# A hybrid decoder layer on one core: the first head's two weight tiles are multiplied chunk of tokens by chunk of tokens instead of tile by tile

## The chip, the core and the metric

The kernel runs on one core of a Trainium2 chip. The metric is the device time of one execution in microseconds (us). A core has five engines, each with its own in-order instruction queue: TensorE (PE in the profile, with its weight loads shown apart as PEld), VectorE (DVE), ScalarE (ACT), GpSimd (POOL) and SyncE (SP, which here only issues DMAs). They wait for one another by semaphores.

## What is computed

One layer of a hybrid decoder over a prompt of 1024 tokens and 32 sample tokens (8 sequences of 4), 1056 tokens in all, width 1024. The part around the change:

```python
h = _rmsnorm(x, norm1)                       # 1056 x 1024
z = h @ w_in                                 # columns: hq, hf, hi, hog, aq, ak, av, iq, ik, iw, ga, gb
# HGRN2 branch, 4 heads of 128
logf = jnp.logaddexp(jnp.log(lb), jnp.log1p(-lb) + jax.nn.log_sigmoid(hf))
o, s_new = _hgrn2(hq, -jnp.expm1(logf), hi, logf, s0)
o = _rmsnorm(o, hg_norm) * jax.nn.silu(hog)
# then sparse attention with an indexer, two gates, w_o, a squared-ReLU MLP, a last norm
```

For each head the HGRN2 branch takes four products of `h` with 128 columns of `w_in`: `hi` (the input, called `whi` in the trace), `hog` (the output gate, `whog`), `hq` and `hf`.

## The kernel before

**Stages.** The tokens are normed in nine blocks of 128 (the ninth has 32). For each block ACT squares and sums (L205), DVE scales (`ht`, L214), PE transposes the block in eight 128x128 pieces (`hTp`, L218), ACT casts the result into the high part `hh` (L219) and DVE subtracts to get the low part `hl` (L220). `hh` and `hl` hold `h` transposed: 8 slices of the width by 1056 tokens. Then come the four HGRN2 heads, the indexer's scores and the search for the top 256 keys, four heads of sparse attention with the sample tokens' attention beside them, the two branch projections, `w_o`, and the MLP.

**A product.** `proj` (L150) loads a weight tile of 1024 x 128 (`wload`, L132; ACT casts its high part and DVE subtracts the low part), and walks over three chunks of 352 tokens (`CUTS`). For each chunk `gemm3` (L142) issues 24 matmuls, three for each of the 8 slices of the width (high by high, L147; high by low, L148; low by high, L149), into one PSUM bank of the tag `g`, which has two banks. `evac` then empties the bank. Chunk 0 needs the token blocks 0 to 2, chunk 1 blocks 2 to 5, chunk 2 blocks 5 to 8.

**The first head.** The weights of `whi` and `whog` are loaded and split while the blocks are normed (L207, `first_w`). In the loop over heads `proj` is called for `whi` (evacuated by an ACT copy to `vT`, L375), the result is transposed back (`tokp`, L385), and then `proj` is called for `whog` (ACT takes the sigmoid `sgo`, L400, and DVE multiplies it into `sil`, L401). The transposes of the raw input (`xTp`, L233, into a PSUM tag `t` of two banks, copied by ACT at L235) are written between. The PSUM tag `s` (two buffers) serves `hTp`, `tokp` and others.

**What sets the order.** Instructions are not executed in the order of the text. A list scheduler places them on each engine's queue by readiness in its own estimate and by priority (the `tc.high_priority()` blocks go ahead), and each queue then runs strictly in that order. So an instruction that waits holds all those behind it on its engine, and a change in one place can change the order that the scheduler finds much later.

Of the kernel before, what the change touches and what calls it, by code (L numbers as in the profile page):

```python
# [10 lines left out]
F32 = mybir.dt.float32  # L11
# [3 lines left out]
AF = mybir.ActivationFunctionType  # L15
ALU = mybir.AluOpType
# [6 lines left out]
T = NP + NS  # L23
CH = 352
# [13 lines left out]
CUTS = (0, 352, 704, 1056)  # L38
# [14 lines left out]
C_HQ, C_HF, C_HI, C_HOG, C_AQ, C_AK, C_AV, C_IQ, C_IK, C_GA, C_GB = (  # L53
    0, 512, 1024, 1536, 2048, 2560, 3072, 3584, 4096, 4168, 5192)
# [37 lines left out]
def hybrid_step(ctx: ExitStack, tc, x_prompt, x_sample, cache_k, cache_v, cache_idx_k, state_hgrn,  # L92
# [3 lines left out]
    nc = tc.nc  # L96
# [5 lines left out]
    sm = ctx.enter_context(tc.tile_pool(name="sm", bufs=1))  # L102
    up = ctx.enter_context(tc.tile_pool(name="up", bufs=1))
    psum = ctx.enter_context(tc.tile_pool(name="psum", bufs=2, space=PSUM))
    U = Units(up, N_UNITS)

    def ps_g(name):
        return psum.tile([128, 512], F32, name=name, tag="g", bufs=2)

    def ps_t(name):  # L110
        return psum.tile([128, 512], F32, name=name, tag="t", bufs=2)
# [17 lines left out]
    hh = big.tile([128, 8, T], F32R, name="hh", tag="hh")  # L129
    hl = big.tile([128, 8, T], F32R, name="hl", tag="hl")  # L130


    def wload(rows, c0, nk, m, name):
        raw = wp.tile([128, nk, m], F32, name=name + "r", tag="wr", bufs=1)
        nc.sync.dma_start(raw, rows[:, c0:c0 + m].rearrange("(k p) m -> p k m", p=128))
        wh = wp.tile([128, nk, m], F32R, name=name + "h", tag="wh", bufs=2)
        wl = wp.tile([128, nk, m], F32R, name=name + "l", tag="wl", bufs=2)
        with tc.high_priority():
            nc.scalar.copy(wh, raw)  # L139
            nc.vector.tensor_tensor(wl, raw, wh.bitcast(F32), op=ALU.subtract)  # L140
        return wh, wl

    def gemm3(ps, ws, xs):
        n = len(ws)
        for k in range(n):
            (wh, wl), (xh, xl) = ws[k], xs[k]
            nc.tensor.matmul(ps, wh, xh, start=(k == 0), stop=False)  # L147
            nc.tensor.matmul(ps, wh, xl, start=False, stop=False)  # L148
            nc.tensor.matmul(ps, wl, xh, start=False, stop=(k == n - 1))  # L149

    def proj(c0, m, name, evac, after=None, w=None):
        wh, wl = w or wload(w_in[0], c0, 8, m, name)
        for c, (a, b) in enumerate(zip(CUTS, CUTS[1:])):
            sl = slice(a, b)
            ps = ps_g(name)[:m, :b - a]
            gemm3(ps, [(wh[:, k, :], wl[:, k, :]) for k in range(8)],
                  [(hh[:, k, sl], hl[:, k, sl]) for k in range(8)])
            with tc.high_priority():
                evac(ps, sl, c)
            if after:  # L160
                after()

    def rstd_of(ss, n, scale, name):
        rt = sm.tile([128, 3, 9], F32, name=name, tag="rs", bufs=2)
        v, r, t = (rt[:ss.shape[0], a, :n] for a in range(3))
        nc.vector.tensor_scalar(v, ss, scale, EPS, op0=ALU.mult, op1=ALU.add)
        nc.scalar.activation(r, v, AF.Sqrt)
        nc.vector.reciprocal(r, r)

        nc.vector.scalar_tensor_tensor(t, r, -0.5, r, op0=ALU.mult, op1=ALU.mult)  # L170
        nc.vector.tensor_tensor(t, t, v, op=ALU.mult)
        nc.vector.scalar_tensor_tensor(r, t, 1.5, r, op0=ALU.add, op1=ALU.mult)
        return r
# [19 lines left out]
    first_w = None  # L193
    for grp in GROUPS:
# [13 lines left out]
        if not first_w and grp[-1] >= FIRST_W:  # L208
            first_w = [wload(w_in[0], C_HI, 8, 128, "whi"), wload(w_in[0], C_HOG, 8, 128, "whog")]
# [122 lines left out]
    def gate_tile(after=None):  # L332
        w, j = gates.pop(0)

        def ev(ps, sl, c):
            gst = sm.tile([128, CH], F32, name="gst", tag="c352", bufs=2)
            nc.scalar.copy(gst, ps)
            nc.scalar.dma_start(sg_d[w, j][:, sl], gst)
        proj((C_GA, C_GB)[w] + j * 128, 128, "wgt", ev, after)
# [32 lines left out]
    tails = []  # L372
    for h in range(4):
        vT = U.get([128, T], F32, "vT")
        proj(C_HI + h * 128, 128, "whi", lambda ps, sl, c: nc.scalar.copy(vT[:, sl], ps),  # L375
             w=first_w[0] if h == 0 else None)

        vk = U.get([128, 8, 128], F32, "vk")
        vks = sm.tile([32, 128], F32, name="vks", tag="s128", bufs=2)
# [12 lines left out]
        if tails:  # L392
            tail(*tails.pop())

        sil = U.get([128, T], F32, "sil")

        def ev_og(ps, sl, c):
            sg_ = sm.tile([128, CH], F32, name="sgo", tag="c352", bufs=2)
            sg_ = sg_[:, :sl.stop - sl.start]
            nc.scalar.activation(sg_, ps, AF.Sigmoid)  # L400
            nc.vector.tensor_tensor(sil[:, sl], ps, sg_, op=ALU.mult)  # L401
        proj(C_HOG + h * 128, 128, "whog", ev_og, w=first_w[1] if h == 0 else None)
        q = U.get([128, T], F32, "q")
        proj(C_HQ + h * 128, 128, "whq", lambda ps, sl, c: nc.scalar.copy(q[:, sl], ps))
        b = U.get([128, T], F32, "b")
# [68 lines left out]
        for li, B in enumerate(LEVELS):  # L474
# [23 lines left out]
            ps = ps_t("lev")  # L498
# [56 lines left out]
    for t0, t1_ in ((0, 5), (5, 9)):  # L555
        ps = ps_t("tkp")
# [47 lines left out]
    for i in range(2, 8):  # L604
# [3 lines left out]
        w = L if small else L // 2  # L608
# [3 lines left out]
        for kind in (DOTS_S if small else DOTS_L):  # L612
# [8 lines left out]
            for ps in bk:  # L621
                h, o = todo.popleft()
# [410 lines left out]
    for step in SEQ.split():  # L1033
        op, n = step[0], int(step[1:] or 0)
# [139 lines left out]
    for j in (0, 4, 1, 5, 2, 6, 3, 7):  # L1174
        x1 = X1[j] = U.get([128, T], F32, f"x1_{j}")
        nc.gpsimd.dma_start(x1, xT_d[j])
        wh, wl = wload(w_o[0], j * 128, 8, 128, "wo")
# [3 lines left out]
        for c in range(NCH):  # L1181
            sl = slice(c * CH, (c + 1) * CH)
            ps = ps_g("po")[:, :CH]
# [11 lines left out]
        if j == 7:  # L1195
# [3 lines left out]
            for c in range(4):  # L1199
                sl = slice((c % 2) * TH + (c // 2) * TC, (c % 2) * TH + (c // 2 + 1) * TC)  # L1200
# [5 lines left out]
        if j >= 4:  # L1206
            kp = j - 4
            dst = {}
            for n_, q in enumerate(ORDER):
                w = kp * 7 + n_  # L1210
# [67 lines left out]
    def bank(i, q, c):  # L1278

        if q in ("P1", "P6", "P7", "P4"):  # L1280
            if (i, 0) not in BANK:
                t = ps_s("pua")
                BANK[i, 0] = [t[:, e, :TC] for e in range(2)]
            return BANK[i, 0][c]
        k = 1 if q == "P2" else 2
        if (i, k) not in BANK:
            BANK[i, k] = [(ps_g("pub") if k == 1 else ps_t("puc"))[:, :TC] for _ in range(2)]
        return BANK[i, k][c]
# [24 lines left out]
    for g, (i, q) in enumerate(SEVEN):  # L1313
        if q == "P2":
            hd[i] = [U.get([128, T], F32, f"hd{e}") for e in range(2)]
        for c in range(2):
            sl = slice(c * TC, (c + 1) * TC)
            s2 = slice(TH + c * TC, TH + (c + 1) * TC)
            product(g, c, (3,) if g in (0, 1, 3) else range(4))
            ps, u1 = bank(i, q, c), 3 * (i % 2)  # L1320
# [24 lines left out]
        if q in ("P2", "P7", "P4", "P3"):  # L1345
            e, sl = {"P2": (0, LO), "P7": (1, HI), "P4": (1, LO), "P3": (0, HI)}[q]
# [61 lines left out]
    for fb in range(8):  # L1408
        rows = w_down[0, fb * 512:(fb + 1) * 512, :]
        if fb < 7:  # L1410
            nxt = []
            for m2 in range(4):
                wh, wl = wd0 if fb == m2 == 0 else wload(rows, m2 * 256, 4, 256, "wd")
# [15 lines left out]
        else:  # L1429

            ws = []
            for m2 in range(4):
                raw = wp.tile([128, 4, 256], F32, name="wdr", tag="wr", bufs=1)
                nc.sync.dma_start(raw, rows[:, m2 * 256:(m2 + 1) * 256].rearrange("(k p) m -> p k m", p=128))
                wh = U.get([128, 4, 256], F32R, "wdh")
                wl = U.get([128, 4, 256], F32R, "wdl")
# [40 lines left out]
```

## Time and profile before

| | before |
|---|---|
| median of 3 runs (lowest to highest) | 1827.23 us (1824.29 to 1831.37) |
| the profiled execution's own time | 1815.77 us |
| its span, first to last instruction | 1814.1 us |
| mean granted TensorE clock | 0.987 of full speed |
| busy: PE, DVE, ACT, POOL | 96%, 63%, 43%, 10% of the span |

The profile is of one execution. Its rows give the start of an instruction or a group in us from the span's start, its length, the engine, the line, and the operands by the program's names. An engine's idle time before a group, and the instruction that ended it, stand in square brackets. The granted clock is 1 at 2.4 GHz and 0.5 at 1.2 GHz; values between are means over a stretch that has both.

### The profile page before, as it was taken

The numbers are of one execution on the slowest core, as the hardware profiler recorded it, in microseconds if no ns is written. First come the engines' busy times: TensorE is split into PE (matmuls) and PEld (weight loads), VectorE is DVE, ScalarE is ACT, GpSimd is POOL, SyncE is SP. The second block draws the span as 40 slices with busy tenths as digits, with TensorE's granted clock in tenths as the row PEclk, the third lists the DMA queues.
The fourth block names the chain that finished last, engine by engine and source line by source line (L and its number), as shares of the span: only waits on it lengthen the run. The fifth ranks groups of instructions, "written<-read, shape, count | busy, mean of one in ns | idle before, by whom it ended". The sixth has DMA issues, their size and how long they took to land.

```text
span 1814.1 us, 29069 instructions
## 1 busy us (share of the span) xinstructions
PE 1745.5 (96%) x11644; PEld 1689.5 (93%) x11644; DVE 1143.2 (63%) x2550; ACT 772.0 (43%) x1362; POOL 186.3 (10%) x212
## 2 busy tenths in 40 slices
PE   5999999999999999989999999999999999999997
PEld 5999999999999988877899999999999899999997
DVE  7185584746899897956647569655565634444435
ACT  5456475245577823244523455444444401111112
POOL 1100000023000014641100230000000000000000
PEclk9999999899999999989999999999999999999999
DMA  4421111231233224551553232233223712222212
GB/s 151 134 60 48 49 55 48 61 93 47 72 85 95 70 83 129 172 180 43 162 161 108 95 121 92 95 129 120 95 95 132 264 55 86 94 95 95 95 47 96
DMA packets 135847, 181.78 MB, mean 100 GB/s; under 512 B 9056, under 2 KB 111232, under 8 KB 135712
## 3 DMA queue, kind: packets, MB, share of 16 engines
q1 hardware_dynamic: 115232, 125.88, 21.6%
q0 software_dynamic: 13424, 44.87, 8.2%
q10 hardware_dynamic: 7056, 9.18, 1.4%
q8 instruction: 91, 1.49, 0.3%
q14 instruction: 44, 0.36, 0.1%
HBM read 128.96 MB, written 48.11 MB: 98 GB/s over the span
## 4 chain that ended last, share of the span: by engine, by line
PE 82%; DMA 6%; DVE 5%; issue 3%; POOL 2%; ACT 2%; SPq 0%; DVEq 0%; ACTq 0%; POOLq 0%
PE pua L1297 10%; PE pd L147 6%; PE pd L149 6%; PE pd L148 6%; PE puc L1297 5%; PE pub L1297 2%; PE lev L506 2%; PE wgt L147 2%; PE wgt L149 2%; PE wgt L148 2%; DMA qb<-q_d 2%; PE po L149 2%; DMA hdn<-hid_d 2%; PE po L148 2%; PE po L147 2%
## 5 line engine op out<-in xcount | busy, mean ns | idle before, releaser
L147 PE MATMUL pd<-hdn,wdh 128*128 128x352 f32 (+3 forms) x672 | 219.5, 327 | 3.2 <-DVE x L1405 3.1
L148 PE MATMUL pd<-hdn,wdh 128*128 128x352 f32 (+3 forms) x672 | 216.4, 322 | 0.0
L149 PE MATMUL pd<-hdn,wdl 128*128 128x352 f32 (+3 forms) x672 | 216.3, 322 | 0.0
L1405 DVE TENSOR_TENSOR x<-x,pd 128x352 f32<-128x352 f32 (+3 forms) x192 | 99.5, 519 | 177.7 <-PE pd L149 177.6
L147 PEld LDWEIGHTS pd<-hdn,wdh 128*128 128x128 f32 x672 | 126.7, 189 | 5.8 <-DVE x L1405 4.5
L148 PEld LDWEIGHTS pd<-hdn,wdh 128*128 128x128 f32 x672 | 126.9, 189 | 1.2
L149 PEld LDWEIGHTS pd<-hdn,wdl 128*128 128x128 f32 x672 | 126.6, 188 | 1.3
L147 PE MATMUL wgt<-hh,wgth 128*128 128x352 f32 x384 | 127.3, 331 | 0.0
L149 PE MATMUL wgt<-hh,wgtl 128*128 128x352 f32 x384 | 125.3, 326 | 0.0
L148 PE MATMUL wgt<-hl,wgth 128*128 128x352 f32 x384 | 125.1, 326 | 0.0
L139 ACT CAST wdh<-wdr 128x1024 fp32r<-128x1024 f32 x28 | 29.4, 1049 | 222.3 <-PE pd L148 210.9
L1297 PE MATMUL pua<-h2P,wuP 128*128 128x264 f32 x672 | 102.7, 284 | 0.0
L750 ACT ACTIVATE jkA<-sc,bstg 128x1024 bf16<-128x1024 bf16 (+5 forms) x93 | 87.1, 937 | 19.6 <-DVE bstg L769 6.8
L1297 PEld LDWEIGHTS pua<-h2P,wuP 128*128 128x128 f32 x672 | 90.4, 188 | 0.0
L745 DVE TENSOR_SCALAR_CACHE_REDUCE jkD<-sc,bstg 128x768 bf16<-128x768 f32 (+3 forms) x96 | 84.4, 879 | 1.1
L1297 PE MATMUL pua<-h2a,wuP 128*128 128x264 f32 x480 | 79.1, 286 | 1.7 <-ACT uu L1323 1.7
L147 PEld LDWEIGHTS wgt<-hh,wgth 128*128 128x128 f32 x384 | 72.6, 189 | 2.5 <-issue 1.7
L148 PEld LDWEIGHTS wgt<-hl,wgth 128*128 128x128 f32 x384 | 72.7, 189 | 1.4 <-issue 0.5
L149 PEld LDWEIGHTS wgt<-hh,wgtl 128*128 128x128 f32 x384 | 72.6, 189 | 1.4 <-issue 0.8
L1323 ACT COPY uu<-pua 128x264 f32<-128x264 f32 x96 | 36.3, 378 | 80.7 <-PE pua L1297 80.7
L1297 PEld LDWEIGHTS pua<-h2a,wuP 128*128 128x128 f32 x480 | 66.7, 188 | 3.0 <-ACT uu L1323 2.8
L1248 DVE TENSOR_TENSOR wuP<-ws,wuP 128x512 fp32r<-128x512 f32 x64 | 43.8, 687 | 39.8 <-ACT wuP L1247 39.4
(782 smaller groups left out, 4969.6 us busy)
## 6 DMA issues: line engine op xcount, KB each, us to landing
hid_d<-hd SPq DMA_DIRECT2D x32, 528.0 KB, 3.0
wu<-in_w_up_dram SPq DMA_DIRECT2D x32, 512.0 KB, 4.5
wdr<-in_w_down_dram SPq DMA_DIRECT2D x32, 512.0 KB, 3.4
hdn<-hid_d SPq DMA_DIRECT2D x28, 528.0 KB, 6.2
sg_d<-gst ACTq DMA_DIRECT2D x48, 176.0 KB, 2.0
wgtr<-in_w_in_dram SPq DMA_DIRECT2D x16, 512.0 KB, 4.2
qb<-q_d POOLq DMA_DIRECT2D x16, 512.0 KB, 4.6
wasg<-sg_d SPq DMA_DIRECT2D x8, 528.0 KB, 4.2
```

The costliest lines, as they stand in the source:

```text
L139: nc.scalar.copy(wh, raw)
L147: nc.tensor.matmul(ps, wh, xh, start=(k == 0), stop=False)
L148: nc.tensor.matmul(ps, wh, xl, start=False, stop=False)
L149: nc.tensor.matmul(ps, wl, xh, start=False, stop=(k == n - 1))
L506: nc.tensor.matmul(ps[:, c * 64:(c + 1) * 64], E[:, c * 128:(c + 1) * 128], mov(c * 128, (c + 1) * 128), start=True, stop=True)
L745: nc.vector.tensor_scalar(jkD[:, 0, :L], SC[i], s if isinstance(s, float) else s[:, a:a + 1], 0.0, op0=op, op1=ALU.add, accum_out=out[:, a ...
L750: nc.scalar.activation(jkA[:, 0, :(i + 1) * 128], src(i), AF.Sign, bias=thr[:, a:a + 1], accum_out=cnt[:, a:a + 1])
L1248: nc.vector.tensor_tensor(w[:, 1], src, w[:, 0].bitcast(F32), op=ALU.subtract)
L1297: nc.tensor.matmul(ps, w[:, a, k], x[:, b, sl], start=(q in "P1P2P5" and k == n_ == 0), stop=(k == 3 and n_ == 2), skip_group_check=True)
L1323: nc.scalar.copy(uu[c][:, {"P1": u1, "P6": 1, "P7": 2}[q]], ps)
L1405: nc.vector.tensor_tensor(x1[:, sl], x1[:, sl], ps, op=ALU.add)
```

## The change

A new function `proj_two` takes a list of products and walks over the three chunks in the outer loop and over the products in the inner one. For head 0 it is called with `whi` and `whog`, so the text has `whi` chunk 0, `whog` chunk 0, `whi` chunk 1, `whog` chunk 1, `whi` chunk 2, `whog` chunk 2. The other three heads keep the order they had. The same matmuls, evacuations and transposes are issued, and `sil` is allocated earlier for head 0.

```diff
+    def proj_two(ms):
+
+        for c, (a, b) in enumerate(zip(CUTS, CUTS[1:])):
+            sl = slice(a, b)
+            for name, evac, (wh, wl) in ms:
+                ps = ps_g(name)[:, :b - a]
+                gemm3(ps, [(wh[:, k, :], wl[:, k, :]) for k in range(8)],
+                      [(hh[:, k, sl], hl[:, k, sl]) for k in range(8)])
+                with tc.high_priority():
+                    evac(ps, sl, c)
...
         vT = U.get([128, T], F32, "vT")
-        proj(C_HI + h * 128, 128, "whi", lambda ps, sl, c: nc.scalar.copy(vT[:, sl], ps),
-             w=first_w[0] if h == 0 else None)
+
+        def ev_og(ps, sl, c):
+            sg_ = sm.tile([128, CH], F32, name="sgo", tag="c352", bufs=2)
...
+            nc.scalar.activation(sg_, ps, AF.Sigmoid)
+            nc.vector.tensor_tensor(sil[:, sl], ps, sg_, op=ALU.mult)
+
+        def ev_i(ps, sl, c):
+            nc.scalar.copy(vT[:, sl], ps)
+        if h == 0:
+            sil = U.get([128, T], F32, "sil")
+            proj_two([("whi", ev_i, first_w[0]), ("whog", ev_og, first_w[1])])
+        else:
+            proj(C_HI + h * 128, 128, "whi", ev_i)
...
-        proj(C_HOG + h * 128, 128, "whog", ev_og, w=first_w[1] if h == 0 else None)
+        if h:
+            sil = U.get([128, T], F32, "sil")
+            proj(C_HOG + h * 128, 128, "whog", ev_og)
```

The order that the scheduler finds is another on three engines. PE's queue before, where the first chunk of `whi` ends: the transposes of blocks 5 and 6 (`hTp` x16), one matmul of chunk 1, then the transposes of block 7.

```order
L148 MATMUL whi<-hl,whih 128x352
L149 MATMUL whi<-hh,whil 128x352
L218 MATMUL hTp<-ident,ht 128x128 x16
L147 MATMUL whi<-hh,whih 128x352
L218 MATMUL hTp<-ident,ht 128x128 x8
L148 MATMUL whi<-hl,whih 128x352
```

PE's queue now, from the end of the first chunk of `whog`. Ahead of these rows stand the 23 remaining matmuls of `whi` chunk 0, nine of `whog` chunk 0, the transposes of blocks 5 and 6, and eleven more of `whog`.

```order
L147 MATMUL whog<-hh,whogh 128x352
L148 MATMUL whog<-hl,whogh 128x352
L149 MATMUL whog<-hh,whogl 128x352
L244 MATMUL xTp<-idr,xt 128x128 x8
L229 MATMUL hTp<-ident,ht 128x128 x8
L244 MATMUL xTp<-idr,xt 128x128 x4
L147 MATMUL whi<-hh,whih 128x352
L148 MATMUL whi<-hl,whih 128x352
```

Fourteen matmuls of `whog` and eight transposes of the raw input now stand between the transposes of block 6 and those of block 7; before, one matmul stood there.

ACT's queue before, from the casts of blocks 4 to 7 on (`lbt` is the exponential for the forget gate's lower bound, `xT` the copies of the raw input's transposes):

```order
L219 CAST hh<-hTp 128x8x128 x4
L253 ACT_TABLE_LOAD
L253 ACTIVATE lbt<-lbt 128x8
L219 CAST hh<-hTp 128x8x32
L235 COPY xT<-xTp 128x512
L375 COPY vT<-whi 128x352
```

ACT's queue now, at the same place:

```order
L230 CAST hh<-hTp 128x8x128 x3
L390 ACT_TABLE_LOAD
L390 ACTIVATE sgo<-whog 128x352
L246 COPY xT<-xTp 128x512
L394 COPY vT<-whi 128x352
L246 COPY xT<-xTp 128x512
L264 ACT_TABLE_LOAD
L264 ACTIVATE lbt<-lbt 128x8
L230 CAST hh<-hTp 128x8x128
L246 COPY xT<-xTp 128x512
L230 CAST hh<-hTp 128x8x32
```

The sigmoid of `whog` chunk 0 with a table load, two copies of `xT`, the copy that frees `whi`'s bank and a second table load now stand ahead of block 7's cast. A third load stands further back, ahead of the second sigmoid; before, the two loads at this place and at the first sigmoid were all.

Between PE's 2754th and 4522nd instruction of 11047, which takes in the attention stage, the order differs again, by the scheduler's choice alone. POOL's queue before, in the sample tokens' scores (`qb` by DMA is a fetch of two query rows, `qb` by TENSOR_TENSOR their multiplication with cached keys, `kpg` a gather of keys):

```order
L892 TENSOR_TENSOR qb<-kpg,qb 128x1024
L875 DMA qb<-q_d 128x1024
L892 TENSOR_TENSOR qb<-kpg,qb 128x1024
L319 DMA kpg<-in_cache_k_dram,ids 128x512 x2
L892 TENSOR_TENSOR qb<-kpg,qb 128x1024
L875 DMA qb<-q_d 128x1024 x2
```

POOL's queue now, at the same place:

```order
L910 TENSOR_TENSOR qb<-kpg,qb 128x1024 x2
L893 DMA qb<-q_d 128x1024
L330 DMA kpg<-in_cache_k_dram,ids 128x512 x2
L893 DMA qb<-q_d 128x1024
L910 TENSOR_TENSOR qb<-kpg,qb 128x1024 x2
L893 DMA qb<-q_d 128x1024
```

Two multiplications now stand back to back, and the fetch that stood between them comes after the second. On SP's queue two loads each change places with a neighbour (`waqr` with `wgtr`, `war` with `wasg`). After that the order is as before.

## Rows read from the trace of the kernel before

**Rows 1.** The page's first part: busy time and share of the span of each engine.

```profile
PE 1745.5 (96%) x11644; PEld 1689.5 (93%) x11644; DVE 1143.2 (63%) x2550; ACT 772.0 (43%) x1362; POOL 186.3 (10%) x212
```

**Rows 2.** Busy time by stretches of 50 us. Columns: the stretch, its length, then for PE, PEld, DVE, ACT and POOL the busy us (and instructions), the granted clock, the share of DMA time and GB/s.

```profile
50.00:100.00 50.00, 50.00 (x330) 49.41 (x329) 15.84 (x22) 25.21 (x40) 7.08 (x8) 1.00 0.42 119
...
300.00:350.00 50.00, 48.23 (x303) 45.17 (x301) 43.05 (x77) 25.75 (x34) 4.20 (x7) 0.90 0.29 77
...
600.00:650.00 50.00, 50.00 (x320) 49.46 (x319) 43.87 (x181) 39.43 (x80) 7.25 (x6) 1.00 0.28 79
...
800.00:850.00 50.00, 37.66 (x209) 28.13 (x208) 25.13 (x86) 20.50 (x40) 5.78 (x8) 0.90 0.21 69
```

**Rows 3.** The same view in short stretches of the start.

```profile
27.00:31.00 4.00, 3.77 (x30) 3.51 (x28) 3.90 (x8) 1.14 (x2) 0.18 (x1) 1.00 0.50 131
31.00:34.00 3.00, 0.46 (x2) 0.24 (x3) 3.00 (x9) 0.79 (x1) 0.00 (x0) 1.00 0.00 0
34.00:38.00 4.00, 4.00 (x20) 4.00 (x21) 4.00 (x22) 2.51 (x3) 1.15 (x2) 0.62 0.01 4
38.00:40.00 2.00, 2.00 (x17) 1.78 (x15) 1.98 (x24) 0.00 (x0) 0.00 (x0) 0.91 0.00 0
...
48.00:60.00 12.00, 12.00 (x85) 11.92 (x85) 2.27 (x3) 6.84 (x12) 2.65 (x3) 1.00 0.62 177
```

**Rows 4.** What PE waited for between 24 and 60 us: us in total, times, longest.

```profile
PE hTp L218 <- DVE scr L291: 2.5, 1, 2.5
PE whi L147 <- ACT hh L219: 0.2, 1, 0.2
```

**Rows 5.** PE in order of time at the start: start us, length us, line, operation, out<-in, count.

```profile
23.67 1.58 PE L218 MATMUL hTp<-ident,ht 128*128 128x128 f32 x8
...
25.41 0.32 PE L147 MATMUL whi<-hh,whih 128*128 128x352 f32 x1
...
25.57 0.32 PE L148 MATMUL whi<-hl,whih 128*128 128x352 f32 x1
...
28.79 1.91 PE L218 MATMUL hTp<-ident,ht 128*128 128x128 f32 x16
...
30.93 0.43 PE L147 MATMUL whi<-hh,whih 128*128 128x352 f32 x1 [0.23 <-ACT hh L219]
33.90 1.06 PE L218 MATMUL hTp<-ident,ht 128*128 128x128 f32 x8 [2.54 <-DVE scr L291]
...
35.25 0.49 PE L147 MATMUL whi<-hh,whih 128*128 128x352 f32 x1
35.54 0.49 PE L148 MATMUL whi<-hl,whih 128*128 128x352 f32 x1
...
39.48 0.68 PE L218 MATMUL hTp<-ident,ht 32*128 32x32 f32 x8
40.09 1.09 PE L233 MATMUL xTp<-idr,xt 128*128 128x128 f32 x8
...
41.66 0.60 PE L233 MATMUL xTp<-idr,xt 128*128 128x128 f32 x4
```

**Rows 6.** ACT in order of time at the start, same columns.

```profile
22.34 1.03 ACT L139 CAST whogh<-whogr 128x1024 fp32r<-128x1024 f32 x1
...
29.86 1.93 ACT L219 CAST hh<-hTp 128x1024 fp32r<-128x1024 f32 x2 [3.56 <-PE hTp L218]
35.00 1.02 ACT L219 CAST hh<-hTp 128x1024 fp32r<-128x1024 f32 x1 [3.21 <-PE hTp L218]
36.04 1.28 ACT L253 ACT_TABLE_LOAD   x1
37.33 0.21 ACT L253 ACTIVATE lbt<-lbt 128x8 f32<-128x8 f32 x1
...
40.78 0.59 ACT L235 COPY xT<-xTp 128x512 f32<-128x512 f32 x1 [0.21 <-PE xTp L233]
41.26 0.46 ACT L375 COPY vT<-whi 128x352 f32<-128x352 f32 x1
```

**Rows 7.** DVE in order of time at the start, same columns.

```profile
30.03 2.47 DVE L214 SCALAR_TENSOR_TENSOR ht<-xt,rsx,g 128x1024 f32<-128x1024 f32 x2
...
32.55 1.20 DVE L220 TENSOR_TENSOR hl<-hTp,hh 128x1024 fp32r<-128x1024 f32 x1
...
40.60 0.42 DVE L220 TENSOR_TENSOR hl<-hTp,hh 128x256 fp32r<-128x256 f32 x1 [0.43 <-ACT hh L219]
...
54.49 0.53 DVE L401 TENSOR_TENSOR sil<-whog,sgo 128x352 f32<-128x352 f32 x1 [5.19 <-ACT sgo L400]
```

**Rows 8.** Busy time in two stretches of 10 us of the attention stage, columns as in the second group.

```profile
660.00:670.00 10.00, 6.26 (x36) 5.33 (x35) 9.86 (x24) 0.37 (x1) 0.00 (x0) 0.99 0.22 64
670.00:680.00 10.00, 9.65 (x35) 7.80 (x36) 9.07 (x24) 2.84 (x7) 0.00 (x0) 0.67 0.00 0
```

**Rows 9.** DVE in order of time in the sample tokens' scores, three of the sixteen multiplications of fetched queries with keys (the first, the seventh and the last).

```profile
692.08 1.22 DVE L891 TENSOR_TENSOR pr<-kpg,qb 128x1024 f32<-128x1024 f32 x1 [3.23 <-DMA qb<-q_d]
...
730.58 1.23 DVE L891 TENSOR_TENSOR pr<-kpg,qb 128x1024 f32<-128x1024 f32 x1 [1.21 <-DMA qb<-q_d]
...
788.44 1.23 DVE L891 TENSOR_TENSOR pr<-kpg,qb 128x1024 f32<-128x1024 f32 x1
```

**Rows 10.** POOL in order of time at the same place, the first of its sixteen multiplications.

```profile
693.39 2.40 POOL L892 TENSOR_TENSOR qb<-kpg,qb 128x1024 f32<-128x1024 f32 x1 [4.27 <-DVE mx L863]
```

More of the change, by code (lines that the diff above doesn't have):

```diff
@@ L374, in hybrid_step @@
         vT = U.get([128, T], F32, "vT")
-        proj(C_HI + h * 128, 128, "whi", lambda ps, sl, c: nc.scalar.copy(vT[:, sl], ps),
-             w=first_w[0] if h == 0 else None)
+        def ev_og(ps, sl, c):
+            sg_ = sm.tile([128, CH], F32, name="sgo", tag="c352", bufs=2)
+            sg_ = sg_[:, :sl.stop - sl.start]
+            nc.scalar.activation(sg_, ps, AF.Sigmoid)
[7 more added lines that the diff above has]
+            proj(C_HI + h * 128, 128, "whi", ev_i)
         vk = U.get([128, 8, 128], F32, "vk")
@@ L393, in hybrid_step @@
             tail(*tails.pop())
[L395 to L401, printed above, removed]
-        proj(C_HOG + h * 128, 128, "whog", ev_og, w=first_w[1] if h == 0 else None)
+        if h:
+            sil = U.get([128, T], F32, "sil")
+            proj(C_HOG + h * 128, 128, "whog", ev_og)
         q = U.get([128, T], F32, "q")
```

## The prediction, made before the changed kernel ran

> **What bounds the kernel now.** I read the page's busy times first: PE is busy for 96% of the span, every other engine far less [rows 1]. The stretches of 50 us then say where PE is not: it is full from 50 us on, nearly full around 300 us, full up to 650 us, and short in the attention stage, most at 800 to 850 us [rows 2]. Before 650 us time is therefore gained only by taking work from PE or by filling a hole in PE's time. The change takes no work away, so I looked for holes where it acts. From 27 to 40 us the short stretches show three things: PE idles 4.00 - 3.77 = 0.23 us and 3.00 - 0.46 = 2.54 us, and then, though always busy, has a granted clock of 0.62 for 4 us and 0.91 for 2 us [rows 3]. The waits name the hole: 2.5 us ahead of a transpose `hTp` [rows 4]. From 48 to 60 us PE has no hole [rows 3].
>
> Who holds PE? The waiting transposes are those of token block 7 (33.90 us) [rows 5]. They need a buffer that DVE frees by `hl` of block 5, from 32.55 to 33.75 us [rows 7]. The wait table names another DVE instruction, which started beside the end of that one; by the program's buffers it is `hl`. DVE was late because the scaling of blocks 7 and 8 stood ahead of it, from 30.03 to 32.50 us [rows 7]. Behind the waiting transposes stood all of `whi` chunk 1, which needs block 5 as well. `whog` chunk 0, whose three blocks were long there, stood a whole tile further back.
>
> **What the change does at the start, in its own time.** A full-clock matmul of 352 columns takes 25.57 - 25.41 = 0.16 us from start to start, one at the half clock 35.54 - 35.25 = 0.29 us [rows 5].
>
> PE. The first `whog` matmul stands ahead of block 4's transposes and waits for its weights' cast, done at 22.34 + 1.03 = 23.37 us [rows 6]; those transposes started at 23.67 us [rows 5], so I book 0.1 us of loss. The rest of `whi` chunk 0 ends at 28.79 + 0.1 = 28.9 us. Nine matmuls of `whog` (1.44) bring 30.3 us, the transposes of blocks 5 and 6 (1.91 [rows 5]) 32.2 us, fourteen more of `whog` (2.24) 34.5 us. By then block 7's buffer is free, and PE goes on without a gap: eight `xTp` (1.09), block 7 (1.06), four `xTp` (0.60) [rows 5] give 37.3 us, where `whi` chunk 1 starts. These lengths overlap a little with what follows, so that is a late estimate; some 36.8 us is an early one.
>
> So the hole of 2.54 and the one of 0.23 us are filled, and the clock has no idle stretch ahead of which it fell. What the low clock cost is 4 x 0.38 + 2 x 0.09 = 1.70 us [rows 3]. The sum is 0.23 + 2.54 + 1.70 - 0.1 = **4.4 us**.
>
> ACT. Two waits are new. The first is for the bank of `whi` chunk 1, free when `vT` chunk 0 is copied. That copy stands behind the casts of blocks 5 and 6, a table load and the sigmoid of `whog` chunk 0. The casts (1.93) start when block 5 is transposed, near 31.3 us, and end at 33.3; the load (1.28) ends at 34.5 [rows 6]; the sigmoid waits for PE's 34.5 us and, taken as long as the `vT` copy of its shape (0.46), ends at 35.1; `xT` (0.59) at 35.7, `vT` (0.46) at 36.2 us [rows 6]. PE wants the bank at 36.8 to 37.3 us: covered by 0.6 us or more.
>
> DVE. The second is for the bank of `whog` chunk 1, free when DVE has made `sil` chunk 0, and that is the tight one. On ACT one more `xT`, the second load and `lbt` end at 36.2 + 0.59 + 1.28 + 0.21 = 38.3 us, block 7's cast at 39.3 [rows 6]. DVE's queue stops at a step that needs `lbt`. Behind it stand 11 small steps, `hl` of block 7, 10 small ones, `hl` of block 8, 5 small ones and `sil`. DVE did 24 mostly such steps in 1.98 us, 0.08 each [rows 3]. So: 38.3 + 0.9 = 39.2, wait for the cast to 39.3, 1.20 for `hl`, 0.8, 0.42, 0.4, and 0.53 for `sil` [rows 7] give 42.7 us. PE gets there after fourteen `whi` (2.24), block 8 (0.61 to the next start), two times four `xTp`, ten `whi` (1.6), two of `tokp` (0.2, estimated by the transposes' 1.06 for eight) and eight `xTp`: from 36.8 with short estimates 43.0 us, from 37.3 with full lengths 44.2 us [rows 5]. The cover is 0.3 to 1.5 us. I book nothing; if it is gone PE waits, with its whole queue behind.
>
> One rule speaks against this. ACT shows `hh` from 35.00 to 36.02, the load from 36.04 to 37.32, and the exponential from 37.33 us [rows 6]: a load costs 1.28 us and no more. The Trainium skill (ScalarE: Activation LUTs, What ACT_TABLE_LOAD costs) adds a drain of about 1380 ns to each switch. By that page two drains would put `sil` at 45.5 us, and PE would wait 1.3 to 2.5 us: a gain of 1.9 to 3.1 us in place of 4.4. By the row I keep 4.4.
>
> The third load falls after 44 us, where ACT works 6.84 of 12 us [rows 3], and is covered. Block 7's cast goes from 35.0 to 38.3 us, but its first user is `whi` chunk 2, after 46 us. The `xT` stores by POOL and the two swapped loads of SP feed work tens of us later. The evacuations are the same ones.
>
> **Whether it lasts.** After the start PE is full to 650 us [rows 2], the one visible gap lying between 300 and 350 us (48.23 of 50), where PE waited on DVE work that PE itself feeds; it moves along. Nothing is tied to an absolute time, so 4.4 us arrive at the attention stage.
>
> **What the change does there without meaning to.** The order of PE, ACT, DVE and POOL is reshuffled in the attention stage, roughly from 480 to 900 us. No row shows the new order, so I bound it. On the side of gain: at 660 to 680 us PE idles 3.74 + 0.35 = 4.1 us, and at a granted clock of 0.67 loses 10 x 0.33 = 3.3 us more [rows 8]. The new queue keeps more query matmuls between the waits there. If all that was on the path, **7.4 us** are the bound. But DVE is busy 9.86 and 9.07 of 10 us in these stretches [rows 8], and PE's loss is mostly a shadow of DVE's work, which is the same. On the side of loss: three fetches of queries now stand behind a second multiplication of 2.40 us [rows 10], **7.2 us** if each is on the path. Against it: the sixteen steps had the back-to-back pattern in the first six and the mixed one after, and ran at (730.58 - 692.08) / 6 = 6.42 and (788.44 - 730.58) / 9 = 6.43 us [rows 9], so the pattern made no difference. I take **0**, nearest to those two paces, and keep both bounds for the range.
>
> **The sum.** On the profiled execution's own 1815.77 us (1.67 us lie around the span) 4.4 us less are 1811.4 us. The median of the runs, 1827.23, lies 11.46 us above that; I take the difference as it is: **1822.8 us**, 0.24% less. Some 0.5%, 9.1 us, is what a measurement of this kernel can tell from no change.
>
> **Rivals.**
> *The wait moves instead of going.* `sil` chunk 0 comes 2.5 us after PE wants the bank, and the clock falls again for the 1.70 us of [rows 3]: 4.4 - 4.2 leaves 0.2, **1827.0 us**. For it speak the two loads and the small DVE steps ahead of `sil`; against it the cover worked out above. Another form is the same in time: the change does in effect nothing.
> *Slower.* One mechanism: the query fetches on POOL behind the second multiplication. It decides from the point where DVE waits for a fetch in each of the three places: 7.2 - 4.4 = +2.8, **1830.0 us**. For it: DVE does wait for such fetches, 3.23 and 1.21 us in two of the rows. Against it: the equal paces [rows 9].
> *Faster.* The hole at 660 to 680 us closes and was on the path: 4.4 + 7.4, **1815.4 us**. For it: the new order puts filler there, and the sample queries that start the next chain are produced by that filler. Against it: DVE's load.
>
> **How the numbers follow.** Forecast 0.55, by its own bounds 1819.5 to 1826 us; the moved wait 0.13; faster 0.17; slower 0.08; a reshuffle larger than my bounds 0.07, to either side alike. The range of 8 in 10 leaves out that last case and half of the outer edge of the faster and slower ones: **1814.0 to 1830.5 us**. Faster by over 0.5% means below 1818.1 us: the faster rival and half of the last case, 0.20. Slower by over 0.5% means above 1836.4 us: half of the last case and a little of the slower rival, 0.05. Within 0.5% is the rest, 0.75.
>
> **What would show it.** Right: PE without a gap and at a granted clock of 1.00 from 27 to 40 us; `whog` matmuls between 29 and 35 us; the first `whf` or `lev` rows some 4 us earlier; the same lead at 600 us. Wrong at the start: a PE wait ahead of `whog` chunk 1 at 42 to 46 us, put down to `sil`, with a low clock behind it. Wrong later: a lead that grows or shrinks between 650 and 900 us; then the idle PE in 660 to 680 and 800 to 850 us, and the pace of the sixteen steps, say which rival it was. A lead of 4 us at 600 us with a total that differs by more than 9 us would put the cause into the reshuffle, which I can bound but not order.

## The result, and the profile after

| | before | after |
|---|---|---|
| median of 8 runs each, us | 1826.97 | 1814.56 |
| lowest to highest, us | 1820.90 to 1835.82 | 1810.48 to 1818.81 |
| ratio, with 95% interval | | 0.9927 [0.9907, 0.9947] |
| the profiled execution, us | 1815.77 | 1816.38 |

The changed kernel takes 12.4 us less. The forecast was 4.4 us less. Two executions far out of line, 2154.6 us in e1 and 6056.1 us among the runs of before beside it, stand in the medians below but not in the ratios. The two profiled executions show no gain at all, 1815.77 against 1816.38 us, and why that is belongs to what was learned (last section).

Read in the order of the prediction. The page's busy times answer to [rows 1], and stretches of 50 us to [rows 2]:

```profile
PE 1751.5 (97%) x11644; PEld 1693.3 (93%) x11644; DVE 1143.1 (63%) x2550; ACT 771.7 (43%) x1363; POOL 186.8 (10%) x212
```

```profile
300.00:350.00 50.00, 47.20 (x308) 43.82 (x307) 44.16 (x79) 27.69 (x37) 4.20 (x7) 0.94 0.29 77
...
800.00:850.00 50.00, 43.29 (x250) 33.70 (x249) 26.15 (x87) 22.31 (x43) 5.37 (x8) 0.93 0.23 72
```

The gap at 300 us is still there (2.80 us idle), as the prediction said. At 800 to 850 us PE now has 43.29 busy us where it had 37.66: something changed there that the change did not set out to do.

The start, in the short stretches of [rows 3], with one more stretch ahead:

```profile
23.00:27.00 4.00, 4.00 (x17) 3.79 (x16) 4.00 (x5) 2.50 (x4) 0.00 (x0) 0.50 0.00 0
27.00:31.00 4.00, 4.00 (x26) 4.00 (x26) 3.89 (x8) 0.00 (x0) 0.00 (x0) 0.99 0.48 131
31.00:34.00 3.00, 3.00 (x26) 2.98 (x25) 2.64 (x7) 1.52 (x2) 0.18 (x1) 1.00 0.02 5
34.00:38.00 4.00, 4.00 (x33) 3.98 (x32) 3.58 (x21) 3.95 (x7) 0.64 (x1) 1.00 0.00 0
38.00:40.00 2.00, 2.00 (x14) 1.78 (x13) 0.93 (x12) 1.99 (x4) 1.42 (x3) 1.00 0.11 35
```

PE is full from 23 to 40 us. Its clock of 0.50, the lower of its two levels (1.2 GHz), from 23 to 27 us lies ahead of the place where the change acts, and is this execution's: of seven other traces with the new start six have 1.00 there, one 0.82. The table of PE's waits from 24 to 60 us, which had two rows in [rows 4], is now empty. PE in order of time (as [rows 5]):

```profile
31.41 1.91 PE L229 MATMUL hTp<-ident,ht 128*128 128x128 f32 x16
33.07 0.41 PE L148 MATMUL whog<-hl,whogh 128*128 128x352 f32 x1
...
35.23 0.33 PE L149 MATMUL whog<-hh,whogl 128*128 128x352 f32 x1
35.39 1.04 PE L244 MATMUL xTp<-idr,xt 128*128 128x128 f32 x8
36.26 1.04 PE L229 MATMUL hTp<-ident,ht 128*128 128x128 f32 x8
37.14 0.60 PE L244 MATMUL xTp<-idr,xt 128*128 128x128 f32 x4
37.49 0.41 PE L147 MATMUL whi<-hh,whih 128*128 128x352 f32 x1
...
44.09 0.41 PE L147 MATMUL whog<-hh,whogh 128*128 128x352 f32 x1
```

The fourteen `whog` matmuls stand where PE idled, block 7's transposes follow without a wait, and `whi` chunk 1 starts at 37.49 us (36.8 to 37.3 forecast). `whog` chunk 1 starts at 44.09 us, where the prediction put PE's demand for the second bank at 43.0 to 44.2. ACT and then DVE, whose `sil` frees that bank (as [rows 6, 7]):

```profile
34.43 1.28 ACT L390 ACT_TABLE_LOAD   x1
35.72 0.47 ACT L390 ACTIVATE sgo<-whog 128x352 f32<-128x352 f32 x1
...
36.55 0.47 ACT L394 COPY vT<-whi 128x352 f32<-128x352 f32 x1
36.90 0.62 ACT L246 COPY xT<-xTp 128x512 f32<-128x512 f32 x1
37.53 1.28 ACT L264 ACT_TABLE_LOAD   x1
38.82 0.21 ACT L264 ACTIVATE lbt<-lbt 128x8 f32<-128x8 f32 x1
```

```profile
39.97 1.22 DVE L231 TENSOR_TENSOR hl<-hTp,hh 128x1024 fp32r<-128x1024 f32 x1
...
42.91 0.52 DVE L391 TENSOR_TENSOR sil<-whog,sgo 128x352 f32<-128x352 f32 x1
```

`sil` ends at 42.91 + 0.52 = 43.4 us, 0.7 us ahead of PE (forecast 42.7). Both covers held. Each table load is 1.28 us and the activation starts at once behind it (34.43 + 1.28 = 35.71, 37.53 + 1.28 = 38.81): the drain that the Trainium skill (ScalarE: Activation LUTs, What ACT_TABLE_LOAD costs) adds to a switch does not appear in these rows.

So the start did what was forecast. The attention stage did not. Its stretches of [rows 8]:

```profile
660.00:670.00 10.00, 10.00 (x61) 9.52 (x61) 9.93 (x17) 2.46 (x5) 3.00 (x2) 1.00 0.43 128
670.00:680.00 10.00, 8.24 (x51) 7.47 (x50) 9.86 (x27) 1.89 (x5) 0.00 (x0) 1.00 0.20 52
```

PE idles 1.8 us in place of 4.1, and its clock stays at 1.00. The steps of [rows 9], first, seventh and last:

```profile
695.08 1.23 DVE L909 TENSOR_TENSOR pr<-kpg,qb 128x1024 f32<-128x1024 f32 x1 [5.66 <-DMA qb<-q_d]
...
733.58 1.23 DVE L909 TENSOR_TENSOR pr<-kpg,qb 128x1024 f32<-128x1024 f32 x1 [1.36 <-DMA qb<-q_d]
...
791.16 1.22 DVE L909 TENSOR_TENSOR pr<-kpg,qb 128x1024 f32<-128x1024 f32 x1
```

Their pace is (791.16 - 695.08) / 15 = 6.41 us, (788.44 - 692.08) / 15 = 6.42 before [rows 9]: equal, as argued. What moved is where the sixteen begin, seen below.

### The profile page after: what moved, and what is told of

It is laid out like the page before. It is cut to its first block, busy times and chain, and to the rows that moved or that the text cites. A ratio compares the mean times of both kernels' runs of the same rounds, so it can differ in the third digit from the quotient of the medians.

```text
span 1814.7 us, 29072 instructions
## 1 busy us (share of the span) xinstructions
PE 1751.5 (97%) x11644; PEld 1693.3 (93%) x11644; DVE 1143.1 (63%) x2550; ACT 771.7 (43%) x1363; POOL 186.8 (10%) x212
## 4 chain that ended last, share of the span: by engine, by line
PE 48%; DMA 5%; DVE 4%; issue 3%; POOL 1%; ACT 1%; SPq 0%; DVEq 0%; ACTq 0%; POOLq 0%
PE pua L1315 10%; PE pd L147 6%; PE pd L149 6%; PE pd L148 6%; PE puc L1315 5%; PE pub L1315 2%; PE po L149 2%; PE po L148 2%; PE po L147 2%; DMA hdn<-hid_d 2%; DMA qb<-q_d 2%; DMA vpg<-in_cache_v_dram,ids 1%; PE wap L147 1%; PE wap L149 1%; PE wap L148 1%
## 5 line engine op out<-in xcount | busy, mean ns | idle before, releaser
L1315 PE MATMUL pua<-h2P,wuP 128*128 128x264 f32 x672 | 102.8, 284 | 0.0
```

The costliest lines, as they stand in the source:

```text
L1315: nc.tensor.matmul(ps, w[:, a, k], x[:, b, sl], start=(q in "P1P2P5" and k == n_ == 0), stop=(k == 3 and n_ == 2), skip_group_check=True)
```

## Experiments: start and order apart

Two theories. BOTH: the start is worth about 4 us and the scheduler's new order in the attention stage about 8. START: all of it comes from the start. They can be parted, because the scheduler took one of two orders there, depending, it seems, on the time at which it believes the stage begins: a few idle matmuls far ahead, whose results are overwritten, turn one into the other.

```diff
             ps = ps_g(name)[:m, :b - a]
+            for _ in range(N if (name, c) == ("wik", 0) else 0):
+                nc.tensor.matmul(ps, wh[:, 0, :], hh[:, 0, sl], start=True, stop=True)
             gemm3(ps, [(wh[:, k, :], wl[:, k, :]) for k in range(8)],
```

**e1**, before unchanged. 

> The kernel before once more, against itself. Every theory expects a ratio of 1.000 with an interval of some 0.3% to either side. What it is to tell: how the span of a run goes with its mean granted clock when nothing is changed, since the profiled execution of before (1815.77 us) lies 11 us below the median of its runs (1827 us). If the runs of before differ by the clock alone, spans should fall on one line against the clock.


Measured: 1831.85 us, ratio 1.0010 [0.9988, 1.0031]. Over the 32 runs of before beside it the time falls by 11 us for each 0.01 of the mean granted clock (correlation -0.77), with 2.6 us of scatter about the line: most of the spread goes with the clock, not all.

**e2**, before with N = 5: old start, new order. 

> The start of before with an attention stage in the order of after: five idle matmuls (0.16 us each, 0.8 us in all) ahead of the product wik shift the scheduler's estimate so that it finds the order of after there (PE's order agrees to 0.998, before and after to 0.939). Theory START (the start gives all of the 12.4 us): ratio 1.0004, 1827.8 us. Theory BOTH (the start gives the forecast 4.4 us, the order of the attention stage the other 8): 1827.0 - 8 + 0.8 = 1819.8 us, ratio 0.996. Theory ORDER (the order gives all): 1815.4 us, ratio 0.9936.


Measured: 1821.58 us against 1828.27, ratio 0.9951 [0.9927, 0.9976]. The order alone, with 0.8 us of idle matmuls to carry, gains 6.7 us.

**e3**, after with N = 20: new start, old order. 

> The start of after with an attention stage in the order of before: twenty idle matmuls (3.2 us in all) ahead of wik (PE's order agrees to 0.996 with before). Theory START: 1827.0 - 12.4 + 3.2 = 1817.8 us, ratio 0.995. Theory BOTH: 1827.0 - 4.4 + 3.2 = 1825.8 us, ratio 0.9993. Theory ORDER: 1830.2 us, ratio 1.0018.


Measured: 1820.30 us, ratio 0.9953 [0.9938, 0.9968]. That is the number of START, not that of BOTH.

**e4**, before with N = 20: old start, old order, same padding as e3. 

> Control: the start of before, the attention stage in the order of before (PE's order agrees to 0.996), and the same twenty idle matmuls as in the run with the new start. All theories: 1827.0 + 3.2 = 1830.2 us, ratio 1.0018. If it is much off, the idle matmuls cost something else than their time, and the other two runs have to be read against this one: new start with old order less this control is what the start alone is worth.


Measured: 1826.74 us, ratio 0.9995 [0.9977, 1.0013]. Twenty idle matmuls (20 x 0.16 = 3.2 us) cost nothing that is seen; in its trace they stand at 310.8 to 314.0 us, ahead of PE's gap of [rows 2]. So e3 is to be read against e4: 6.4 us for the start alone.

START falls by e2, ORDER (1.0018) by e3, and the low price of the padding explains why e3 came out below BOTH's number: each half gains by itself.

**e5**, after with only the first chunk interleaved. PE's order from the attention stage on is the changed kernel's.

```diff
-        for c, (a, b) in enumerate(zip(CUTS, CUTS[1:])):
+        for m, c in ((0, 0), (1, 0), (0, 1), (0, 2), (1, 1), (1, 2)):
+            a, b = CUTS[c], CUTS[c + 1]
...
-            for name, evac, (wh, wl) in ms:
+            for name, evac, (wh, wl) in ms[m:m + 1]:
```

> The changed kernel, with only the first chunk interleaved: whi chunk 0, whog chunk 0, then whi chunks 1 and 2 and whog chunks 1 and 2. PE's order from the attention stage on is that of the changed kernel. Theory CHUNK 0 (the gain at the start is whog chunk 0 standing in the hole ahead of the transposes of block 7, nothing else): the time of the changed kernel within 1.5 us, 1813 to 1816 us at a median of before of 1827, ratio 0.993; the first U product of head 0 near 103.6 us, as in the changed kernel. Rival ALL CHUNKS (interleaving chunks 1 and 2 spreads the evacuations and is part of the gain): 2 to 4 us slower than the changed kernel, ratio 0.994 to 0.995, first U at 105 to 107 us.


Measured: 1811.87 us against 1819.67, ratio 0.9950 [0.9930, 0.9970]; first `U` at 102.8 us (103.6 in after). The ratio is inside ALL CHUNKS's numbers and not at CHUNK 0's 0.993, so by the ratio alone CHUNK 0 missed. But the first `U` is CHUNK 0's, and that is the row which the start alone sets; and e9, the whole change on another chip, has no lower a ratio, 0.9954. Up to the first `U`, chunk 0 does the start's work; the two kernels were not run on one chip.

**e9** and **e10**: after, and before with N = 5, on one chip, so that they differ in the start alone (and 0.8 us of idle matmuls).


> The changed kernel once more, beside e10 on one chip. Theory BOTH (the start is worth some 4 us, the new order of the attention stage some 8): ratio to before 0.992 to 0.9945. The difference to e10 is the price of the start with the order of the attention stage held: 4 us less than e10 less its 0.8 us of idle matmuls. Rival ORDER ALONE (the lead of the start is lost before the end): the same time as e10 within 1 us.

> The kernel before with 5 idle matmuls (0.8 us) ahead of the product wik, which turn the order of the attention stage into that of the changed kernel, as in e2, beside e9 on one chip. Theory BOTH: ratio to before 0.9945 to 0.997, and 3 to 5 us above e9. Rival ORDER ALONE: the time of e9 within 1 us.


Measured: e9 1809.21 us, ratio 0.9954 [0.9935, 0.9974]; e10 1813.53 us, ratio 0.9979 [0.9960, 0.9997], with before at 1816.19. The start is worth 4.3 us less 0.8, 3.5 us (4.3 if the idle matmuls cost nothing, as in e4). ORDER ALONE, at most 1 us, does not fit, though the two intervals overlap from 0.9960 to 0.9974. But both ratios are nearer to 1 than BOTH said: the order alone gains 2.7 + 0.8 = 3.5 us here, not 8.

The first products `U` of head 0 in both traces (times of first and last start):

```profile
L455 PE MATMUL U<-vk,KT x64: 271/275/328, 102.4 to 325.0; 128*128 128x128 f32 x64
```

```profile
L439 PE MATMUL U<-vk,KT x64: 271/275/328, 107.6 to 326.2; 128*128 128x128 f32 x64
```

Over all traces the first `U` starts at 105.9 to 107.6 us with the old start (six, mean 106.8) and at 102.4 to 103.6 us with the new one (eight, mean 103.0): the start is worth 3.8 us.

## Experiments: what the new order gains by

The place is the query product `waq` of the last head and what follows it. PE of e1, old order:

```profile
686.17 2.50 PE L841 MATMUL S<-kT,qT 128*128 128x512 f32 x4 [3.27 <-DVE mx L845]
689.03 0.66 PE L147 MATMUL waq<-hh,waqh 128*128 128x352 f32 x1 [0.35 <-ACT qT L975]
689.49 0.49 PE L148 MATMUL waq<-hl,waqh 128*128 128x352 f32 x1
689.78 0.49 PE L149 MATMUL waq<-hh,waql 128*128 128x352 f32 x1
...
697.18 0.83 PE L859 MATMUL po<-pT,vt 128*128 128x128 f32 x6
697.85 0.60 PE L853 MATMUL pTp<-ident,s__6513 128*128 128x128 f32 x4
698.56 0.28 PE L967 MATMUL qsp<-ident,qsT 128*32 128x128 f32 x1
```

PE of after:

```profile
676.00 1.30 PE L859 MATMUL S<-kT,qT 128*128 128x512 f32 x4
679.07 0.43 PE L147 MATMUL waq<-hh,waqh 128*128 128x352 f32 x1 [1.76 <-ACT qT L993]
...
684.19 3.04 PE L859 MATMUL S<-kT,qT 128*128 128x512 f32 x8
687.07 0.27 PE L985 MATMUL qsp<-ident,qsT 128*32 128x128 f32 x1
```

In the old order an `S` waits 3.27 us for DVE with the last third of `waq` behind it, the clock is half afterwards (689.78 - 689.49 = 0.29 us a matmul), and `qsp` stands behind four more transposes. `qsp` turns the last head's query rows; ACT copies them (`qts`), they go to `q_d`, and the sixteen steps fetch from there. By tile, in us:

| | first `po` to `qts` | `qts` to `sS` |
|---|---|---|
| old order: before, e1, e3, e4 | 27.1, 26.4, 26.6, 27.5 | 152.1, 154.7, 151.3, 149.4 |
| new order: after, e2, e5, e9, e10 | 20.8, 20.9, 20.8, 20.8, 20.9 | 149.2, 147.6, 147.5, 150.4, 151.5 |

(`po` is the first product of a softmax with values in the stage, `sS` the transposes of the sample scores behind the sixteenth step.) The copy comes 6.1 us earlier (means 26.9 and 20.8), and the stage to `sS` is 8.7 us shorter in the traces (178.8 and 170.1). PE's rows account for nearly all of the 6.1 us: between the first `po` and `qsp`, with the same 72 matmuls of `waq`, PE idles 4.09 us at a mean clock of 0.87 in before and e1, and 1.76 us at 1.00 in after and e9. That is 2.3 us of idle time and 26 x 0.13 = 3.4 us of clock. Theory CHAIN: what counts is when that copy leaves. Rival HOLE: PE's idle time and clock count, whenever the copy leaves.

**e6** and **e7**: the last head's query product one gate tile earlier in the program, in after and in before.

```diff
-SEQ = "Q0 L G G Q1 G G G G G G Q2 G G P A1 A0 q3 S G1 k1 G1 A2 G1 G1 G1 G1 A3 E"
+SEQ = "Q0 L G G Q1 G G G G G G Q2 G q3 G P A1 A0 S G1 k1 G1 A2 G1 G1 G1 G1 A3 E"
```

> The changed kernel, with the query product of the last head taken one gate tile (72 matmuls, 11.5 us) earlier in the program, and that gate tile after it. Theory CHAIN (the attention stage ends a fixed time, some 149 us, after the query rows of the last head are copied to be fetched, because 16 steps of about 6 us each and the value steps hang on that copy; the new order gained by an earlier copy): the copy comes about 10 us earlier, the first step can use only what DVE leaves, the 5.7 us that it waited for the fetch there, so 4 to 6 us less than the changed kernel, about 1809 us, ratio 0.990. Rival HOLE (the gain of the new order is PE's closed hole and its full clock between 660 and 680 us; when the copy leaves makes no difference): the time of the changed kernel, 1814.5 us, ratio 0.993, or more if the missing gate tile opens the hole again.


Measured: 1807.88 us, ratio 0.9936 [0.9913, 0.9959]; 4.0 us under e5 of the same chip, with intervals that overlap. The first step came 5.7 us earlier than in e5 (676.33, 682.04), but the last one at the same time (777.40, 777.45): fifteen steps took 101.1 us in place of 95.4. CHAIN's fixed time fails on this side: here an earlier copy gained nothing by the last step.

> The kernel before, with the query product of the last head taken one gate tile earlier, as in e6. Theory CHAIN: the copy of the last head's query rows leaves 10 to 16 us earlier than in the kernel before, the first of the 16 steps starts as early as DVE's work allows, and the stage is 8 to 11 us shorter: about 1818 us, ratio 0.995, with the hole of the start unchanged. Rival HOLE: gains only if PE has no hole left between 660 and 690 us; with a hole there 1827 us, ratio 1.000.


Measured: 1807.74 us, ratio 0.9937 [0.9914, 0.9960], 11.9 us under before, a little past CHAIN's 8 to 11. From the last `U` to `sS` its trace has 497.3 us, 508.5 in before, 497.7 in e5. PE's hole is gone too (19.07 and 20.00 busy us of 20 from 660 to 680 and from 680 to 700, at a granted clock of 1.00), so e7 does not part the theories. It does not show the start's gain either: e6 and e7 differ in the start, and in the order that the scheduler finds, and their medians are 0.1 us apart (1807.88 and 1807.74), each ratio with some 4 us to either side. In the traces e6 leads by 3.0 us at the first `U` (102.9 and 105.9), and e7's stretch from the last `U` to `sS` is 2.9 us shorter (497.3 and 500.2); why is open.

**e8** and **e11**: one more, and four more, transfers between the copy and the fetch, PE's order around it kept. The edit of e11, without the declaration of `q_x` and the branch of the other heads:

```diff
+        if h == 3:
+            nc.sync.dma_start(q_x[0], qts)
+            for a in range(3):
+                nc.sync.dma_start(q_x[a + 1], q_x[a])
+            nc.sync.dma_start(q_d[:, h, :], q_x[3])
```

> The changed kernel, with the query rows of the last head stored to a second array in memory first and copied from there, one more transfer between the copy on ACT and the first fetch; PE's order around it is kept. Theory CHAIN: the first of the 16 steps starts later by that transfer, some 2 to 4 us, DVE has nothing to put there, and the whole is that much slower than the changed kernel: 1817 to 1819 us, ratio 0.994 to 0.9955. Rival HOLE: no difference, 1814.5 us, ratio 0.993.


Measured: 1812.58 us, ratio 0.9959 [0.9934, 0.9984], 0.7 us over e5: too little to tell.

> The changed kernel with four more transfers between the copy of the last head's query rows and their fetch. One more took 9.91 - 7.99 = 1.9 us from the copy to the first step in the traces of e8 and e5, so the first step starts some 7.7 us later. Theory CHAIN: the stage ends 6 to 8 us later, 1820 to 1822 us at a median of before of 1827, ratio 0.996 to 0.9975; PE runs dry before the value steps for that much longer. Rival HOLE (only PE's hole at 660 to 680 us counts): the time of e9.


Measured: 1816.76 us, ratio 0.9999 [0.9981, 1.0018], 7.6 us over e9. ACT's copy and the first step in e9, and in e11:

```profile
676.77 0.26 ACT L988 COPY qts<-qsp 32x128 f32<-32x128 f32 x1
```

```profile
684.59 1.23 DVE L909 TENSOR_TENSOR pr<-kpg,qb 128x1024 f32<-128x1024 f32 x1 [5.77 <-DMA qb<-q_d]
```

```profile
674.11 0.26 ACT L989 COPY qts<-qsp 32x128 f32<-32x128 f32 x1
```

```profile
690.68 1.23 DVE L910 TENSOR_TENSOR pr<-kpg,qb 128x1024 f32<-128x1024 f32 x1 [5.16 <-DMA qb<-q_d]
```

From copy to first step 7.82 us became 16.57, 8.75 more, and the runs are 7.6 us longer, while PE from 660 to 680 us is as busy as in e9 (18.24 us in both, at 1.00). HOLE as the whole cause falls: a later first step costs time with the hole unchanged. How much is less sure. PE's order is that of e9 up to 690 us and another from there to 799 us (e8's too departs at 690 us), so the delay is not tested alone. From the copy to `sS` the trace of e11 has only 3.8 us more than that of e9 (154.2 and 150.4), and these two profiled executions end at the same time (spans of 1807.3 us), e11's having lost 3.2 us less ahead of the stage.

Where it is paid: PE of e1, and of after, where the work that covers the chain runs out.

```profile
819.27 0.27 PE L853 MATMUL pTp<-ident,s__7434 128*128 128x128 f32 x1
827.38 0.80 PE L859 MATMUL po<-pT,vt 128*128 128x128 f32 x2 [7.84 <-ACT pT L856]
```

```profile
809.18 0.27 PE L871 MATMUL pTp<-ident,s__7434 128*128 128x128 f32 x1
813.44 0.80 PE L877 MATMUL po<-pT,vt 128*128 128x128 f32 x2 [3.98 <-ACT pT L874]
```

PE waits for `pT`, the transposed softmax that ACT copies. That copy stands in ACT's queue behind the second cast `vsh` of gathered values. The gathers `vpg` stand in POOL's queue behind its sixteenth multiplication (806.29 us in e1), and the second cast waits for one of them. POOL and ACT of e1:

```profile
808.86 1.04 POOL L319 DMA_INDIRECT vpg<-in_cache_v_dram,ids  x1 [0.17 <-issue]
```

```profile
824.67 1.04 ACT L932 CAST vsh<-vpg 128x1024 fp32r<-128x1024 f32 x1 [8.41 <-DMA vpg<-in_cache_v_dram,ids]
...
827.06 0.27 ACT L856 COPY pT<-pTp 128x128 f32<-128x128 f32 x1 [0.40 <-ACT gst L337]
```

7.84 us became 3.98. In all nine traces of the table PE goes on 21.9 to 23.2 us after the sixteenth step starts on DVE, and its wait there is 7.8 to 8.1 us with the old order and 3.8 to 5.0 with the new one.

**e12**: one gate tile taken from ahead of `q3` to the end of the gates.

```diff
-SEQ = "... Q2 G G P A1 A0 q3 S G1 k1 G1 A2 G1 G1 G1 G1 A3 E"
+SEQ = "... Q2 G P A1 A0 q3 S G1 k1 G1 A2 G1 G1 G1 G1 G1 A3 E"
```

> The changed kernel with one gate tile (72 matmuls, 11.5 us) taken from ahead of the last head's query product to the end of the gate tiles, where PE has run dry while it waits for the value steps. Theory CHAIN: the copy of the query rows leaves earlier by up to 11 us, but DVE has the sixteen steps' first place free only 5.7 us earlier, and PE's queue has the same work, so 3 to 6 us less than e9. Rival HOLE: the work that filled PE between 660 and 680 us is gone from there, so the hole opens again and the time is 4 to 8 us more than e9.


Measured: 1828.27 us, ratio 1.0049 [1.0028, 1.0071], 19 us over e9: both missed, HOLE in size only. Its stretches of [rows 8]:

```profile
660.00:670.00 10.00, 2.44 (x7) 1.72 (x8) 9.83 (x24) 0.42 (x2) 0.00 (x0) 0.56 0.02 6
670.00:680.00 10.00, 9.65 (x42) 7.70 (x41) 9.56 (x24) 4.19 (x10) 0.00 (x0) 0.75 0.00 0
```

The gate tile had filled the time in which DVE (9.83 and 9.56 of 10 us) could not yet feed `S`. Without it PE idles 7.9 us at a low clock, the copy comes 349.4 us after the last `U` in place of 350.2, not 11 us earlier, and the tile's 11.5 us are still to be done behind `sS` (gate matmuls from 836 to 910 us: 34.89 busy us, 18.92 in e9). Against e9 the trace has 503.3 - 500.6 = 2.7 us more from the last `U` to `sS` and 994.8 - 980.1 = 14.7 us more from there to the end, 17.4 in all, of which the tile's 11.5 us explain the larger part; another 5.6 us stand in this trace ahead of the last `U`, where both programs are alike. So hole and chain are hardly two rivals: the hole lies in PE's queue ahead of `qsp`, and filling it is what brings the copy forward.

## Why the prediction was wrong

**The start, 4.4 us: right in kind and nearly in size.** Hole, covers, order and times are in the rows above; 3.8 us by the first `U`, 3.5 and 6.4 us by the runs. Within it, the clock's 1.70 us were taken for a sure consequence of the hole. They are not. In all six traces of the old start block 7's transposes begin at 33.9 to 34.0 us. In three of them (before, e2, e10) PE had idled 2.47 to 2.67 us just ahead, the granted clock from 34 to 38 us is 0.60 to 0.66, and the first `U` comes at 107.5 to 107.6 us. In the other three (e1, e4, e7) PE came later and idled 1.24 to 2.04 us, the clock is 1.00, and the first `U` comes at 105.9 to 106.1. So the start is worth 3.0 or 4.6 us by execution.

**Whether it lasts: mostly.** The traces of e9 and e10 part by 5.2 us at the first `U` and by 2.3 us at the first `po` (655.94, 658.28), with different clocks in between; the medians end 4.3 us apart. Between e6 and e7 nothing of it is seen in the medians, within their intervals.

**The moved wait: did not come.** No PE wait from 24 to 60 us. **The slower rival: did not come.** The pace is equal to 0.01 us.

**The step that failed: "I take 0" for the reshuffle.** Measured: 3.5 and 7.5 us by runs (e10, e2; the 0.8 us of idle matmuls added), 8.7 us by traces. The step asked whether the sixteen steps would be faster. They were not, and that was shown correctly. It did not ask when they start. The sample queries are named in the faster rival ("produced by that filler"), with the right place and a bound of 7.4 us, and its 1815.4 us are 0.8 from the result; it had 0.17. That it came so near is in part luck: 5.7 of the 7.4 us went, and beside the same change e9 gains 7.0 us in all. The argument against it, that PE's loss is a shadow of DVE's equal work, overlooked that `qsp` stood behind PE's wait in its queue and that PE ends the stage waiting for what `qsp` starts.

**The sum.** 3.8 for the start and 3.5 to 8.7 for the order are 7.3 to 12.5 us. Measured: 12.4, and 7.0 in e9; the two intervals share 0.9935 to 0.9947, 9.7 to 11.9 us of 1827. The chips differ too: before has 1826.97 us beside after and 1828.27 beside e1 to e4, 1819.67 beside e5 to e8, 1816.19 beside e9 to e12. Whether the order is worth less on the chip of e9, or the runs scatter, is open.

**No better version.** e6 and e7 are the fastest here, at ratios that cannot be told from those of the changed kernel.

## What to carry to other kernels

Where a scheduler works from estimated times, a change of a few us anywhere can turn the order of a stage far behind it; price that as a term of its own, by asking which instruction in the reordered piece starts a long chain, not whether the piece has more or less work. A few idle instructions that turn the order and nothing else let the two be measured apart. Ask of a hole in the fullest engine's time what stands behind it in the queue: here the one at 660 us held back `qsp`, on which sixteen steps and a wait of PE 130 us later hung. There it was worth filling; moving a filler tile of 11.5 us from ahead of it to the end (e12) cost 17 us in the trace and 19 us by the medians.

## What was not expected of the hardware

PE's clock is lower in some stretches in which its rows show it full (the ends of matmuls in them are modelled). In the head stage, stretches 107 to 200 and 410 to 450 us, of before and of e1, the same program:

```profile
107.00:200.00 93.00, 93.00 (x652) 89.13 (x651) 64.92 (x122) 52.98 (x76) 4.37 (x6) 1.00 0.19 54
...
410.00:450.00 40.00, 40.00 (x243) 39.41 (x242) 24.21 (x32) 23.27 (x38) 13.27 (x13) 1.00 0.14 38
```

```profile
107.00:200.00 93.00, 93.00 (x603) 89.13 (x602) 60.16 (x114) 50.36 (x72) 4.38 (x6) 0.93 0.17 48
...
410.00:450.00 40.00, 35.75 (x196) 33.97 (x195) 17.39 (x25) 15.85 (x26) 17.35 (x18) 0.91 0.21 50
```

PE is busy 93.00 of 93.00 us in both, at 1.00 and at 0.93, which is 6.5 us. And PE idled 4.25 us at 410 to 450 us in e1, for nothing that the profile names; it idled 4.0 to 4.7 us there in all five profiled executions on the chips of after and of e1 to e4, and not at all in those of before and e5 to e12. Lines of time against clock through the runs of before give, at a clock of 0.985, 1825.5 us on the chip of e1 to e4 and 1820.4 and 1820.8 us on the two others. That these 5 us are this idle time is near at hand, but not shown.

This is why two profiles 0.6 us apart belong to medians 12.4 us apart. Against before, the profiled execution of after is 3.9 us ahead at the first `U`, loses 14.2 us from there to the first `po` (563.0 and 548.8 us: 5.7 of idle time, 8.5 of clock), gains 9.2 us from there to `sS` (170.0 and 179.2) and 0.5 behind it: 0.6 us more in all. The prediction took its differences inside one profile, where this does no harm; a comparison of two profiles' ends would have been wrong by three times the forecast.
